# Low parts of weights split half a tile later, two products that start without new weights, and a table pass moved behind a convolution's first step, in a hybrid decoder layer on one core

## The chip, the cores and the metric

The kernel runs on one core of a Trainium2 chip. The metric is the device time of one execution in microseconds (us). Engines are named as in the profile: PE multiplies matrices, DVE and ACT work element by element, POOL does side work, SP issues transfers (DMA). Each engine takes its instructions strictly in the order of its own queue, and waits on semaphores for what other engines and transfers deliver.

## The reference

One layer of a decoder trunk on 512 tokens of width 1024, in float32:

```python
h = rms_norm(x, norm_g[0]); proj = h @ w_in          # one projection, split into all branches
y_a = rglru_mixer(lru_x, lru_g, conv_w, conv_b, ...)  # width-4 depthwise conv, gates, linear recurrence, gelu
y_b = nsa_mixer(...)                                  # sparse attention
y_c = gla_mixer(...)                                  # log_alpha = log_sigmoid(lr @ wa2 + ba) / 16, then chunks
merged = gates[0] * (y_a @ w_branch[0]) + gates[1] * (y_b @ w_branch[1]) + gates[2] * (y_c @ w_branch[2])
x = x + rms_norm(merged @ w_out, norm_g[1])
h = rms_norm(x, norm_g[2])
gt, up = jnp.split(h @ w_ffn_in, 2, axis=-1)          # D_FF = 2816
x = x + rms_norm((jax.nn.silu(gt) * up) @ w_ffn_out, norm_g[3])
```

## The kernel before

**Products in split precision.** Every operand of a product is split into a high part in a reduced format (fp32r) and a low part, the rest. A weight tile of 128x1024 comes from DRAM into a buffer `wraw`. ACT copies it into `whi` (the high part, a CAST of about 1.05 us), DVE subtracts that from `wraw` into `wlo` (the low part, about 1.2 us). Then `mm3` (lines 121 to 124) makes three products per pair: high with high (L122), high with low weights (L123), low with high (L124). The pool `wpool` holds three buffers each of `wraw`, `whi` and `wlo`. A `wraw` buffer can be loaded again once DVE has made its low part; a `whi` or `wlo` buffer once PE has used it.

**The recurrent branch.** A loop over `cp` = 0 to 3 handles two of eight channel groups at a time: a projection `px` (`stream_t`), `conv(cp, px)`, a second projection `pgl`, `gate_products(cp)` and a third stream `pm`. `conv` (L988 to L1005) begins on ACT with two scaled copies of `px` into `xc`, goes on with three DVE steps per half (L1000), casts the result to `xh` on ACT (L1002), and subtracts on DVE into `xl` (L1004). The products `rips` of `gate_products` need `xh` and `xl`. Into this loop the logarithms of the GLA decays are woven: `z_products`, `z_exp` and `z_log` run in the `pm` stream of `cp` = 2, and `z_log` (L1072) is four activations that need another activation table. `z_scan` reads their result in the `pgl` stream of `cp` = 3.

**The FFN, first product.** `w_ffn_in` is applied by a seven-product (Strassen-Winograd) scheme, P1 to P7, on quarters. The list `seq` names the products in order, `winograd(s)` does one of them, twelve matmuls into the PSUM bank A, B or C, and `after(op, q)` evacuates it: `keep` is a copy by ACT, `y_half` (L1719) an addition by DVE, `act(q)` (L1751) the product with the silu. `winograd` also prepares weights two tiles ahead: `f_cast(i)` at even s, `f_lo(i)` at odd s. The last two products, P7 and P4 of q = 21, go into the same bank A, so P4 may start only when DVE has read P7 out.

**The FFN, second product.** `w_ffn_out` is applied with another seven-product scheme. The list `stream` orders the weight tiles: a0, b0, a1, b1, ... a10, b10 (`tile_a`, `tile_b`), then pairs of rows and columns. `tile_a(k)` loads two quarters of `w_ffn_out`; `tile_b(k)` loads one block of row sums from `rows_d` and computes the other block on DVE from the raw a tile (L1806). `split_u` casts on ACT and makes the low part on DVE (L1779, L1782). `weights()` hands out the next tile and, by `ahead(i + 3)`, sets up the tile two places later. `use(bank, ...)` does six matmuls of 512 columns with half a tile; every tile serves two such uses. At k = 0, tile a0 is used once between P6 and P7 and once between P7 and P4; from then on step k of the loop (L1933) does two uses of a(k) and two of b(k).

**The order of the work.** PE, DVE, ACT and POOL run in the order in which the program is written (`manual_schedule`); the transfers on SP are put in order by the scheduler. `late` is a list of low parts put off; before the change it is used only near the end (L1996 and L2005). `fetch2(k)` loads a block `r2` for `second(k - 2)` from a pool of three buffers, `gb3` is a vector of gains, and `xr` are the eight loads of the residual (L1970).

```python
    def f_lo(i):
        if i < len(floads):
            raw, hi = fq[i]
            lo = wpool.tile([128, 1024], F32R, name="wlo")
            v_.tensor_tensor(lo, raw, f(hi), op=OP.subtract)
            fq[i] = hi, lo
```

Of the kernel before, what the change touches and what calls it, by code (L numbers as in the profile page):

```python
# [10 lines left out]
F32 = mybir.dt.float32  # L11
# [51 lines left out]
def hybrid_block_kernel(ctx, tc, x, rel_table, norm_g, w_in, conv_w, conv_b, lru_w_gates, lru_b_gates,  # L63
# [924 lines left out]
    def conv(cp, pss):  # L988

        xh = lp.tile([128, 2, S], F32R, name="xh")  # L990
        xl = lp.tile([128, 2, S], F32R, name="xl")
        xc = lp.tile([128, 2, S], F32, name="xc")
        for j, ps in enumerate(pss):
            ct = 2 * cp + j
            a_.activation(xc[:, j], ps, AF.Identity, scale=par[:, 24 + ct:25 + ct], bias=par[:, 32 + ct:33 + ct])
        for j, ps in enumerate(pss):
            ct = 2 * cp + j
            for jj in (2, 1, 0):
                d = 3 - jj
                v_.scalar_tensor_tensor(xc[:, j, d:], ps[:, :S - d], par[:, jj * 8 + ct:jj * 8 + ct + 1],  # L1000
                                        xc[:, j, d:], op0=OP.mult, op1=OP.add)
            a_.copy(xh[:, j], xc[:, j])  # L1002
        for j in range(2):
            v_.tensor_tensor(xl[:, j], xc[:, j], f(xh[:, j]), op=OP.subtract)  # L1004
        L.update(xc=xc, xh=xh, xl=xl)  # L1005
# [76 lines left out]
    for cp in range(4):  # L1082
# [4 lines left out]
        conv(cp, px)  # L1087
# [8 lines left out]
        if cp == 0:  # L1096
            lru_params()
        pm = stream_t(Y[:2], chain(lambda: lru_tanh(cp), *([z_products] if cp == 2 else [])),
                      chain(lambda: lru_exp(cp), *([z_exp, z_log] if cp == 2 else [])))
# [510 lines left out]
    fq = []  # L1610

    def f_cast(i):
        if i < len(floads):
            raw = floads[i]()
            hi = wpool.tile([128, 1024], F32R, name="whi")
            a_.copy(hi, raw)  # L1616
            fq.append([raw, hi])
        else:
            ahead(i - len(floads) + 1)

    def f_lo(i):
        if i < len(floads):
            raw, hi = fq[i]
            lo = wpool.tile([128, 1024], F32R, name="wlo")
            v_.tensor_tensor(lo, raw, f(hi), op=OP.subtract)  # L1625
            fq[i] = hi, lo
# [140 lines left out]
    late = []  # L1767

# [7 lines left out]
    def split_u(raw, n=1024):  # L1776
        hi = wpool.tile([128, 1024], F32R, name="whi")
        lw = wpool.tile([128, 1024], F32R, name="wlo")
        a_.copy(hi[:, :n], raw[:, :n])  # L1779

        def low():
            v_.tensor_tensor(lw[:, :n], raw[:, :n], f(hi[:, :n]), op=OP.subtract)  # L1782

        if late:
            late.append(low)
        else:
            low()
        return hi, lw

# [5 lines left out]
    def tile_a(k):  # L1795

        t = last["a"] = raw_tile()
        sy.dma_start(t[:, 0:512], wsrc(k, 0))
        sy.dma_start(t[:, 512:1024], wsrc(NK + k, 1))
        return split_u(t)  # L1800

    def tile_b(k):

        t, ab = raw_tile(), last["a"]
        sy.dma_start(t[:, 0:512], rows_d[k * 128:k * 128 + 128, 512:1024])
        v_.tensor_tensor(t[:, 512:1024], ab[:, 0:512], ab[:, 512:1024], op=OP.subtract)  # L1806
        return split_u(t)
# [30 lines left out]
    def use(bk, ls, sl, w, hf, k, tts=(0, 1)):  # L1838
        wh, wl = [t[:, hf * 512:hf * 512 + 512] for t in w]
        for tt in tts:  # L1840
            c = slice(tt * 128, tt * 128 + 128)
            mm3(bk[tt], ls[:, 0, sl, c], ls[:, 1, sl, c], wh, wl, k == 0, k == NK - 1)

# [14 lines left out]
    w = weights()  # L1858
    use(p5, LS1[0], 2, w, 1, 0)
# [3 lines left out]
    use(p2, LS1[0], 1, w, 0, 0)  # L1863
    winograd(len(seq) - 1)
    after(*seq[-1])
    a_.activation(cst[:, 2:3], cst[:, 0:1], AF.Sqrt)
# [8 lines left out]
    def fetch2(k):  # L1875
        if k < NK - 1:
            raw2[k] = fr.tile([128, 3, 256], F32, name="r2", bufs=3)
# [42 lines left out]
    def store(tb, hf):  # L1920
# [3 lines left out]
        (sy if hf else a_).dma_start(out[0, tb * 128:(tb + 1) * 128, c], o)  # L1924
# [6 lines left out]
    fetch2(0)  # L1931
    fetch2(1)
    for k in range(NK):  # L1933
# [20 lines left out]
        fetch2(k + 2)  # L1954
# [35 lines left out]
    for p in range(NP - 3):  # L1990
# [3 lines left out]
        if p == 1:  # L1994

            late.append(None)  # L1996
# [7 lines left out]
        if p == 2:  # L2004
            for low in late[1:]:  # L2005
                low()
# [51 lines left out]
```

## Time and profile before

| what | value |
|---|---|
| median of 3 runs | 1201.88 us (1201.55 to 1203.12) |
| the profiled execution, its own time | 1202.26 us |
| its span in the trace | 1200.6 us |
| mean granted PE clock | 0.996 |
| PE busy | 1180.5 us, 98% |
| DVE, ACT, POOL busy | 726.3, 607.0, 256.6 us |

The span runs from the first to the last instruction that the profiler saw; the time also holds what lies around it, 1.7 us here. In the timeline each row gives the start, the duration, the engine, the line of the kernel, the operation, and in brackets how long the engine idled before it and what ended that. In the rows of stretches the columns are: the stretch, its length, the busy time of PE, of PE's weight loads, of DVE, ACT and POOL with their instruction counts, the granted clock of PE (1.00 is full), the DMA share and GB/s.

### The profile page before, as it was taken

The page shows a single profiled execution, that of the slowest core. Times are in us where ns is not written, and L with a number is a line of the kernel's source. Part 1 is how long each engine was busy: PE and PEld are TensorE (multiplying, and loading weights), DVE is VectorE, ACT ScalarE, POOL GpSimd, SP SyncE. Part 2 cuts the span into 40 slices and gives each one's busy share as a digit, 9 for nine tenths or more (in the row PEclk, how much of TensorE's full clock was granted, in tenths as well). Part 3 has the DMA queues.
Part 4 walks back from the last instruction along what each step waited for, and adds up shares of the span by engine and source line. Part 5 has one row for each costly group of instructions (what it writes and reads, how often), then busy time and mean ns, then how long its engine had stood idle before and what let it go on. Part 6 is the DMA issues. An engine that isn't in the chain of part 4 may idle for free. (4 is left out here: it accounts for less than half of the span.)

```text
span 1200.6 us, 19226 instructions
## 1 busy us (share of the span) xinstructions
PE 1180.5 (98%) x7114; PEld 1009.9 (84%) x7114; DVE 726.3 (60%) x1417; ACT 607.0 (51%) x1165; POOL 256.6 (21%) x327
## 2 busy tenths in 40 slices
PE   9999999999999999999999999999999999989996
PEld 7898888888888878888888888887989999987785
DVE  6615556555467769465544353446786777765777
ACT  5326656565387677453434233234455565644553
POOL 1224555566213213222122222200000000000000
PEclk9999999999999999999999999999999999999999
DMA  8872765551469947885487989944246667667753
GB/s 259 236 217 83 195 222 196 179 163 40 115 153 228 246 151 215 202 201 150 132 203 179 212 196 236 214 149 134 85 123 189 207 202 212 197 193 239 244 184 123
DMA packets 203743, 219.30 MB, mean 183 GB/s; under 512 B 29170, under 2 KB 169694, under 8 KB 201424
## 3 DMA queue, kind: packets, MB, share of 16 engines
q1 hardware_dynamic: 189120, 170.87, 46.7%
q0 software_dynamic: 13936, 46.14, 18.3%
q8 instruction: 56, 0.92, 0.3%
q10 hardware_dynamic: 592, 1.05, 0.2%
q14 instruction: 39, 0.32, 0.1%
HBM read 209.83 MB, written 77.41 MB: 239 GB/s over the span
## 5 line engine op out<-in xcount | busy, mean ns | idle before, releaser
L92 DVE TENSOR_TENSOR wlo<-wraw,whi 128x1024 fp32r<-128x1024 f32 x91 | 111.8, 1233 | 113.6 <-ACT whi L91 86.9
L91 ACT CAST whi<-wraw 128x1024 fp32r<-128x1024 f32 x113 | 117.9, 1048 | 118.7 <-PE gps L897 29.6
L870 POOL COPY tick<-whi 128x1 f32<-128x1 f32 x76 | 53.8, 708 | 340.4 <-ACT whi L91 340.4
L894 PE MATMUL gps<-hh,whi 128*128 128x512 f32 x320 | 126.0, 394 | 0.0
L897 PE MATMUL gps<-hl,whi 128*128 128x512 f32 x320 | 124.5, 389 | 0.0
L1625 DVE TENSOR_TENSOR wlo<-wraw,whi 128x1024 fp32r<-128x1024 f32 x67 | 81.9, 1222 | 14.5 <-ACT whi L1616 14.0
L676 DVE COPY psb<-ptp 128x512 f32<-128x512 f32 (+2 forms) x72 | 45.4, 631 | 64.2 <-PE ptp L672 60.5
L637 ACT ACTIVATE p<-p,mx 128x384 f32<-128x384 f32 (+3 forms) x128 | 68.7, 539 | 26.7 <-DVE mx L635 26.5
L894 PE MATMUL gps<-hh,wlo 128*128 128x512 f32 x320 | 79.1, 389 | 0.0
L1616 ACT CAST whi<-wraw 128x1024 fp32r<-128x1024 f32 x67 | 70.3, 1049 | 13.4 <-DMA wraw<-t_d 12.0
L651 POOL TENSOR_TENSOR p<-p,sc 128x256 f32<-128x256 f32 (+3 forms) x64 | 76.5, 1217 | 1.9
L894 PE MATMUL gps<-yh,whi 128*128 128x512 f32 x192 | 74.9, 390 | 0.0
L897 PE MATMUL gps<-yl,whi 128*128 128x512 f32 x192 | 74.7, 389 | 0.0
L122 PE MATMUL gps<-hh,whi 128*128 128x512 f32 (+1 forms) x176 | 73.4, 418 | 0.8 <-DVE hl L316 0.8
L894 PEld LDWEIGHTS gps<-hh,wlo 128*128 128x128 f32 x320 | 60.1, 188 | 12.5
L894 PEld LDWEIGHTS gps<-hh,whi 128*128 128x128 f32 x320 | 60.1, 188 | 12.4
L897 PEld LDWEIGHTS gps<-hl,whi 128*128 128x128 f32 x320 | 60.1, 188 | 12.3
L122 PE MATMUL gps<-whi,hh 128*128 128x512 f32 (+1 forms) x192 | 69.9, 364 | 0.0
L124 PE MATMUL gps<-whi,hl 128*128 128x512 f32 (+1 forms) x192 | 68.1, 354 | 0.0
L123 PE MATMUL gps<-wlo,hh 128*128 128x512 f32 (+1 forms) x192 | 68.0, 354 | 0.0
L124 PE MATMUL gps<-hh,wlo 128*128 128x512 f32 (+1 forms) x176 | 65.7, 374 | 0.0
L123 PE MATMUL gps<-hl,whi 128*128 128x512 f32 (+1 forms) x176 | 65.5, 372 | 0.0
(442 smaller groups left out, 3061.8 us busy)
## 6 DMA issues: line engine op xcount, KB each, us to landing
wraw<-in_w_in_dram SPq DMA_DIRECT2D x44, 512.0 KB, 6.4
t_d<-in_w_ffn_in_dram SPq DMA_DIRECT2D x32, 704.0 KB, 8.0
wraw<-t_d SPq DMA_DIRECT2D x72, 256.0 KB, 3.2
wraw<-in_w_ffn_in_dram SPq DMA_DIRECT2D x70, 256.0 KB, 3.8
wraw<-in_w_in_dram SPq DMA_DIRECT2D x64, 256.0 KB, 4.5
t_d<-in_w_ffn_in_dram POOLq DMA_DIRECT2D x16, 704.0 KB, 9.2
rows_d<-in_w_ffn_out_dram POOLq DMA_DIRECT2D x22, 512.0 KB, 5.2
t_d<-t_d POOLq DMA_DIRECT2D x16, 704.0 KB, 8.2
```

Source lines behind the costliest of these rows:

```text
L91: a_.copy(hi, raw)
L92: lo_eng.tensor_tensor(lo, raw, f(hi), op=OP.subtract)
L122: pe.matmul(ps, lh, rh, start=first, stop=False)
L123: pe.matmul(ps, lh, rl, start=False, stop=False)
L124: pe.matmul(ps, ll, rh, start=False, stop=last)
L637: a_.activation(o, o, AF.Exp, scale=-1.0, bias=mx[:, br, gi:gi + 1], accum_out=sm[:, br, gi:gi + 1])
L651: g_.tensor_tensor(o, o, sc[:, br][:, :, None].to_broadcast([128, 2, n]), op=OP.mult)
L870: g_.tensor_copy(tick, f(hi[:, 0, 0:1]))
L894: pe.matmul(ps[n], part_[:, k, c], ah[:, kk], start=kk == 0 and part_ is h, stop=kk == 7 and part_ is l)
L897: pe.matmul(ps[n], h[:, k, c], al[:, kk], start=False, stop=False)
L1616: a_.copy(hi, raw)
L1625: v_.tensor_tensor(lo, raw, f(hi), op=OP.subtract)
```

## The change

- **z_log.** The four logarithms of the decays and their table load leave the `pm` stream of `cp` = 2. `conv` takes a new argument `then`, called behind its first step (the two scaled copies on ACT), and for `cp` = 3 that is `z_log`.
- **Low parts half a tile later.** `split_u` no longer emits the low part; it appends it to `late`. `lows()` empties `late`. It is called at the start of `f_lo`, at the end of each `use` (after its matmuls), and once ahead of the first `use`.
- **tile_a and tile_b.** `tile_a(k)` now allocates both raw tiles, issues the load for b as well, and subtracts the computed half of b (L1806 before) ahead of the low part of a. `tile_b(k)` only casts.
- **The change of products.** The first two uses take tile a0 as `done[0]`, and `weights()` is no longer called ahead of them. The setting up of b0 moves to the call of `winograd` for P7, that of a1 behind P4.
- **Smaller moves.** The table load for Sqrt with its dummy activation moves from behind P4 to the end of the a/b loop. `fetch2` runs one step later from a pool of four buffers, and the two fetches ahead of the loop go. All stores but the last go out by SP, the last by ACT.

```diff
@@ -985,7 +985,7 @@
         v_.tensor_tensor(gwl, raw, f(gwh), op=OP.subtract)
         L["gw"] = gwh, gwl
 
-    def conv(cp, pss):
+    def conv(cp, pss, then=None):
 
         xh = lp.tile([128, 2, S], F32R, name="xh")
         xl = lp.tile([128, 2, S], F32R, name="xl")
@@ -993,6 +993,8 @@
         for j, ps in enumerate(pss):
             ct = 2 * cp + j
             a_.activation(xc[:, j], ps, AF.Identity, scale=par[:, 24 + ct:25 + ct], bias=par[:, 32 + ct:33 + ct])
+        if then:
+            then()
         for j, ps in enumerate(pss):
             ct = 2 * cp + j
             for jj in (2, 1, 0):
@@ -1084,7 +1086,7 @@
             px = stream_t(hT, lambda: y_split(0), lambda: gate_weights(0))
         else:
             px = stream_t(hT, lru_root, chain(lambda: lru_scan(cp - 1), lambda: gate_weights(cp)))
-        conv(cp, px)
+        conv(cp, px, z_log if cp == 3 else None)
         if cp == 0:
             pgl = stream_t(hT, lambda: y_split(1), chain(lambda: y_split(2), lambda: y_split(3)))
         elif cp == 3:
@@ -1096,7 +1098,7 @@
         if cp == 0:
             lru_params()
         pm = stream_t(Y[:2], chain(lambda: lru_tanh(cp), *([z_products] if cp == 2 else [])),
-                      chain(lambda: lru_exp(cp), *([z_exp, z_log] if cp == 2 else [])))
+                      chain(lambda: lru_exp(cp), *([z_exp] if cp == 2 else [])))
         for j in range(2):
             merge_mul(cp, j, pm[j])
     pq = stream_t(hT, chain(lru_root, lambda: lru_scan(3)))
@@ -1608,8 +1610,15 @@
 
     floads += [lambda s=s: quarters(seq[s:s + 2]) for s in range(0, len(seq), 2)]
     fq = []
+    late = []
+
+    def lows():
+        while late:
+            late.pop(0)()
 
     def f_cast(i):
+        if i >= len(floads) + 2:
+            return
         if i < len(floads):
             raw = floads[i]()
             hi = wpool.tile([128, 1024], F32R, name="whi")
@@ -1619,6 +1628,7 @@
             ahead(i - len(floads) + 1)
 
     def f_lo(i):
+        lows()
         if i < len(floads):
             raw, hi = fq[i]
             lo = wpool.tile([128, 1024], F32R, name="wlo")
@@ -1764,8 +1774,6 @@
 
     HP = []
     raws = [0]
-    late = []
-
     def raw_tile():
         i = raws[0]
         raws[0] += 1
@@ -1781,11 +1789,9 @@
         def low():
             v_.tensor_tensor(lw[:, :n], raw[:, :n], f(hi[:, :n]), op=OP.subtract)
 
-        if late:
-            late.append(low)
-        else:
-            low()
+        late.append(low)
         return hi, lw
+
 
     def wsrc(r, c):
         return dap(w_ffn_out, r * 128 * D + c * 512, [[D, 128], [1, 512]])
@@ -1794,17 +1800,17 @@
 
     def tile_a(k):
 
-        t = last["a"] = raw_tile()
+        t, tb_ = raw_tile(), raw_tile()
         sy.dma_start(t[:, 0:512], wsrc(k, 0))
         sy.dma_start(t[:, 512:1024], wsrc(NK + k, 1))
+        sy.dma_start(tb_[:, 0:512], rows_d[k * 128:k * 128 + 128, 512:1024])
+        v_.tensor_tensor(tb_[:, 512:1024], t[:, 0:512], t[:, 512:1024], op=OP.subtract)
+        last["b"] = tb_
         return split_u(t)
 
     def tile_b(k):
 
-        t, ab = raw_tile(), last["a"]
-        sy.dma_start(t[:, 0:512], rows_d[k * 128:k * 128 + 128, 512:1024])
-        v_.tensor_tensor(t[:, 512:1024], ab[:, 0:512], ab[:, 512:1024], op=OP.subtract)
-        return split_u(t)
+        return split_u(last["b"])
 
     def pair(src):
         def load(p):
@@ -1840,6 +1846,7 @@
         for tt in tts:
             c = slice(tt * 128, tt * 128 + 128)
             mm3(bk[tt], ls[:, 0, sl, c], ls[:, 1, sl, c], wh, wl, k == 0, k == NK - 1)
+        lows()
 
     for s in range(len(seq) - 2):
         winograd(s)
@@ -1855,15 +1862,15 @@
         after(*seq[s])
 
     p2, p5 = [[p.tile([128, 512], F32, name="acc", tag=n) for _ in range(2)] for p, n in ((pa, "a"), (pt, "pt"))]
-    w = weights()
-    use(p5, LS1[0], 2, w, 1, 0)
+    lows()
+    use(p5, LS1[0], 2, done[0], 1, 0)
     y_half(2 * NK - 1, 0, "C", "u2")
     winograd(len(seq) - 2)
     after(*seq[-2])
-    use(p2, LS1[0], 1, w, 0, 0)
+    use(p2, LS1[0], 1, done[0], 0, 0)
     winograd(len(seq) - 1)
     after(*seq[-1])
-    a_.activation(cst[:, 2:3], cst[:, 0:1], AF.Sqrt)
+    weights()
     fictx.close()
     fctx = ExitStack()
     fr = fctx.enter_context(tc.tile_pool(name="ffr", bufs=1, side="right"))
@@ -1874,7 +1881,7 @@
 
     def fetch2(k):
         if k < NK - 1:
-            raw2[k] = fr.tile([128, 3, 256], F32, name="r2", bufs=3)
+            raw2[k] = fr.tile([128, 3, 256], F32, name="r2", bufs=4)
             sy.dma_start(raw2[k], raw2_d[:, k])
 
     def second(k):
@@ -1921,15 +1928,13 @@
         c = slice(hf * 512, hf * 512 + 512)
         o = C[tb][:, c]
         v_.scalar_tensor_tensor(o, gained[tb, hf], rss[tb][1][:, 0:1], xres[tb, hf], op0=OP.mult, op1=OP.add)
-        (sy if hf else a_).dma_start(out[0, tb * 128:(tb + 1) * 128, c], o)
+        (a_ if (tb, hf) == (1, 1) else sy).dma_start(out[0, tb * 128:(tb + 1) * 128, c], o)
 
     def add(o, x_, y, op=OP.add):
         v_.tensor_tensor(o, x_, y, op=op)
 
     p3, p1 = [[pg.tile([128, 512], F32, name="acc", tag="g") for _ in range(2)] for _ in range(2)]
     p4, p6, p7 = p2, p5, p3
-    fetch2(0)
-    fetch2(1)
     for k in range(NK):
         if k:
             w = weights()
@@ -1951,7 +1956,11 @@
             second(k - 2)
         if k == 4:
             second(NK - 1)
-        fetch2(k + 2)
+        if k == 0:
+            fetch2(0)
+        fetch2(k + 1)
+        if k == NK - 1:
+            a_.activation(cst[:, 2:3], cst[:, 0:1], AF.Sqrt)
     for p in range(NP):
         w = weights()
         for k in range(2 * p, min(2 * p + 2, NK)):
@@ -1993,7 +2002,6 @@
             use(p7, LS2[k], 1, w, k % 2, k)
         if p == 1:
 
-            late.append(None)
             ahead(turns[0] + 3)
         if p in (0, 1):
             add(C[2 + p][:, c1], p6[p], C[2 + p][:, c1])
@@ -2002,8 +2010,6 @@
             gain(2 + p, 1)
             mean(2 + p)
         if p == 2:
-            for low in late[1:]:
-                low()
             store(2, 0)
             store(2, 1)
             root(3)
```

ACT around the logarithms, in the recurrent branch at the end of `cp` = 2 and the start of `cp` = 3 (`yf` holds the decays, `a` is the recurrence's root, `gwh` the gate weights, `xc` and `xh` are the convolution's). Before:

```order
L1072 ACT_TABLE_LOAD
L1072 ACTIVATE yf<-yf,cst 128x512 x4
L91 CAST whi<-wraw 128x1024
L1047 ACT_TABLE_LOAD
L1047 ACTIVATE a_4787<-a_4787 128x1024
L91 CAST whi<-wraw 128x1024
L984 CAST gwh<-gwr 128x512
L995 ACTIVATE xc<-gps,par 128x512 x2
L1002 CAST xh<-xc 128x512 x2
```

Of the change:

```order
L91 CAST whi<-wraw 128x1024
L1049 ACT_TABLE_LOAD
L1049 ACTIVATE a_4787<-a_4787 128x1024
L91 CAST whi<-wraw 128x1024
L984 CAST gwh<-gwr 128x512
L995 ACTIVATE xc<-gps,par 128x512 x2
L1074 ACT_TABLE_LOAD
L1074 ACTIVATE yf<-yf,cst 128x512 x4
L1004 CAST xh<-xc 128x512 x2
```

The load of the table and the four logarithms now stand behind `xc` and ahead of `xh`; the two casts of weights, the root and `xc` stand ahead of them.

DVE at the FFN's change of products (`am<-fy,fsg` is `act`, the two `fy` are `y_half` for q = 21, the 512-wide `wraw` row is the computed half of a b tile, L1782 and L1790 are low parts of tiles a and b). Before:

```order
L1782 TENSOR_TENSOR wlo<-wraw,whi 128x1024
L1751 SCALAR_TENSOR_TENSOR am<-fy,fsg 128x512
L1806 TENSOR_TENSOR wraw<-wraw 128x512
L1782 TENSOR_TENSOR wlo<-wraw,whi 128x1024 x2
L1719 TENSOR_TENSOR fy<-wc,u_10699 128x256
L1719 TENSOR_TENSOR fy<-wa,p_10586 128x256
L1806 TENSOR_TENSOR wraw<-wraw 128x512
L1782 TENSOR_TENSOR wlo<-wraw,whi 128x1024
L1751 SCALAR_TENSOR_TENSOR am<-fy,fsg 128x512
```

Of the change:

```order
L1807 TENSOR_TENSOR wraw<-wraw 128x512
L1790 TENSOR_TENSOR wlo<-wraw,whi 128x1024
L1761 SCALAR_TENSOR_TENSOR am<-fy,fsg 128x512
L1729 TENSOR_TENSOR fy<-wc,u_10702 128x256
L1729 TENSOR_TENSOR fy<-wa,p_10586 128x256
L1790 TENSOR_TENSOR wlo<-wraw,whi 128x1024
L1807 TENSOR_TENSOR wraw<-wraw 128x512
L1790 TENSOR_TENSOR wlo<-wraw,whi 128x1024 x2
L1761 SCALAR_TENSOR_TENSOR am<-fy,fsg 128x512
```

The two low parts (b0 and a1) that stood ahead of the additions `fy` stand behind them; ahead of a0's low part there is now b0's subtraction.

SP where the loads of tile a3 stand (`gb` is the vector of gains, `r` the blocks of `fetch2`, `xr` the residual). Before:

```order
L1798 DMA wraw<-in_w_ffn_out_dram 128x512
L1871 DMA gb_10766<-in_norm_g_dram 128x1024
L1878 DMA r_10775<-raw_d 128x768
L1878 DMA r_10777<-raw_d 128x768
L1878 DMA r_10801<-raw_d 128x768
L1799 DMA wraw<-in_w_ffn_out_dram 128x512
L1805 DMA wraw<-rows_d 128x512
L1798 DMA wraw<-in_w_ffn_out_dram 128x512
L1799 DMA wraw<-in_w_ffn_out_dram 128x512
L1970 DMA xr_11337<-x_d 128x512
L1970 DMA xr_11339<-x_d 128x512
L1970 DMA xr_11341<-x_d 128x512
```

Of the change:

```order
L1804 DMA wraw<-in_w_ffn_out_dram 128x512
L1878 DMA gb_10767<-in_norm_g_dram 128x1024
L1885 DMA r_10796<-raw_d 128x768
L1885 DMA r_10798<-raw_d 128x768
L1885 DMA r_10839<-raw_d 128x768
L1805 DMA wraw<-in_w_ffn_out_dram 128x512
L1806 DMA wraw<-rows_d 128x512
L1885 DMA r_10883<-raw_d 128x768
L1804 DMA wraw<-in_w_ffn_out_dram 128x512
L1805 DMA wraw<-in_w_ffn_out_dram 128x512
L1979 DMA xr_11337<-x_d 128x512
L1804 DMA wraw<-in_w_ffn_out_dram 128x512
```

The two halves of a3 still have the gains and three `r` blocks between them; of the eight `xr` loads one, where there were three, is left ahead of a5.

## Rows read from the trace of the kernel before

**Rows 1.** The page's first lines: span, and busy time per engine.

```profile
span 1200.6 us, 19226 instructions
...
PE 1180.5 (98%) x7114; PEld 1009.9 (84%) x7114; DVE 726.3 (60%) x1417; ACT 607.0 (51%) x1165; POOL 256.6 (21%) x327
```

**Rows 2.** Waits of PE: who waited, for whom, total, times, longest.

```profile
PE wa L1707 <- DVE fy L1719: 3.1, 1, 3.1
PE acc L123 <- DVE wlo L1782: 1.3, 3, 0.8
PE rips L123 <- DVE xl L1004: 1.3, 1, 1.3
```

**Rows 3.** Timeline of ACT around the logarithms.

```profile
430.50 1.28 ACT L1072 ACT_TABLE_LOAD   x1
431.79 2.56 ACT L1072 ACTIVATE yf<-yf,cst 128x512 f32<-128x512 f32 x4
434.26 1.03 ACT L91 CAST whi<-wraw 128x1024 fp32r<-128x1024 f32 x1
```

**Rows 4.** Timeline of DVE in the same place.

```profile
435.33 1.23 DVE L92 TENSOR_TENSOR wlo<-wraw,whi 128x1024 fp32r<-128x1024 f32 x1 [4.48 <-ACT whi L91]
...
444.09 4.53 DVE L1000 SCALAR_TENSOR_TENSOR xc<-gps,par,xc 128x511 f32<-128x511 f32 x6
448.54 1.51 DVE L1004 TENSOR_TENSOR xl<-xc,xh 128x512 fp32r<-128x512 f32 x2
```

**Rows 5.** Timeline of PE in the same place.

```profile
436.70 0.39 PE L894 MATMUL gps<-hh,whi 128*128 128x512 f32 x1
...
447.58 0.39 PE L122 MATMUL rips<-xh,gwh 128*128 128x512 f32 x1
449.27 0.50 PE L123 MATMUL rips<-xl,gwh 128*128 128x512 f32 x1 [1.30 <-DVE xl L1004]
...
449.84 0.39 PE L122 MATMUL rips<-xh,gwh 128*128 128x512 f32 x1
```

**Rows 6.** Stretches: all engines, granted clock, DMA share.

```profile
1071.51:1083.68 12.17, 8.97 (x44) 7.53 (x43) 5.34 (x8) 3.84 (x5) 0.00 (x0) 0.86 0.56 181
1079.33:1082.05 2.72, 2.72 (x12) 2.72 (x13) 0.54 (x1) 0.00 (x0) 0.00 (x0) 0.50 0.27 96
1090.51:1128.01 37.50, 35.58 (x145) 26.32 (x144) 24.91 (x26) 17.30 (x20) 0.00 (x0) 1.00 0.81 274
1139.21:1172.14 32.93, 32.93 (x146) 27.02 (x144) 26.44 (x32) 19.34 (x30) 0.00 (x0) 1.00 0.61 197
447.60:452.00 4.40, 3.10 (x14) 2.26 (x13) 3.96 (x6) 3.29 (x5) 1.59 (x2) 1.00 0.00 0
```

**Rows 7.** Timeline of DVE at the FFN's change of products.

```profile
1070.72 1.22 DVE L1782 TENSOR_TENSOR wlo<-wraw,whi 128x1024 fp32r<-128x1024 f32 x1
...
1077.38 1.23 DVE L1782 TENSOR_TENSOR wlo<-wraw,whi 128x1024 fp32r<-128x1024 f32 x1 [1.90 <-ACT whi L1779]
...
1079.19 0.68 DVE L1806 TENSOR_TENSOR wraw<-wraw 128x512 f32<-128x512 f32 x1
...
1086.31 0.69 DVE L1751 SCALAR_TENSOR_TENSOR am<-fy,fsg 128x512 f32<-128x512 f32 x1
```

**Rows 8.** Timeline of ACT in the same place and at tile a3.

```profile
1082.29 0.38 ACT L1742 ACTIVATE fsg<-wa 128x256 f32<-128x256 f32 x1 [4.94 <-PE wa L1707]
1082.69 1.28 ACT L1866 ACT_TABLE_LOAD   x1
...
1095.56 1.05 ACT L1779 CAST whi<-wraw 128x1024 fp32r<-128x1024 f32 x1 [3.60 <-DMA wraw<-in_w_ffn_out_dram]
```

**Rows 9.** Timeline of SP: the second half of tile a3.

```profile
1088.86 0.54 SPq L1799 DMA_DIRECT2D wraw<-in_w_ffn_out_dram  x1
```

**Rows 10.** Timeline of PE: the second product of tiles a0 and a3.

```profile
1071.99 0.50 PE L123 MATMUL acc<-wlo,ls 128*128 128x512 f32 x1
...
1097.92 0.51 PE L123 MATMUL acc<-wlo,ls 128*128 128x512 f32 x1 [0.76 <-DVE wlo L1782]
```

## The prediction, made before the changed kernel had run

> **What bounds the kernel.** The first lines of the page come first [rows 1]: PE is busy 1180.5 of 1200.6 us, so only what PE waits for can be won, and little of it. The list of PE's waits then says for whom [rows 2]. Three entries touch the change: one wait of 3.1 us for `fy`, the additions that free bank A between P7 and P4; three waits, 1.3 us together, for low parts of `w_ffn_out`; one of 1.3 us for `xl` of the convolution. This list keeps only clear gaps. What a place really costs is read from stretches [rows 6]: a quiet one, 1139.21 to 1172.14, has 24 uses (144 products of 512 columns) in 32.93 us, 1.372 us per use. Everything below is measured against that pace.
>
> **Part A, the logarithms.** Behind the third `pgl` stream PE starts `rips` at 447.58; the fourth product starts at 449.84 [rows 5]. Three products should take 3 x 0.229 = 0.69 us and take 2.26, so this place loses 1.58 us. The reason lies well before it: ACT loads a table at 430.50 and does the four logarithms until 434.26, and only then casts a weight tile [rows 3]; DVE idles 4.48 us for that cast [rows 4], and its whole queue (a low part, the root's product, the scans, six convolution steps from 444.09, `xl` at 448.54) comes late.
>
> With the logarithms gone from there, the cast starts at 430.50 and DVE's queue moves 3.76 us forward, unless something else holds it. The candidate is `xc`, which needs the whole of `px`; PE begins the next stream at 436.70 [rows 5], so `xc` runs from about 436.9 to 438.3, while the convolution's steps would start at 444.09 - 3.76 = 440.33: no hold. The moved block, 1.28 + 2.48 = 3.76 us, now occupies ACT from 438.3 to 442.1. Behind it waits `xh`, whose first half needs three steps of DVE, done at 440.33 + 4.53/2 = 442.6. So the block just fits, and the first half of `xl` ends near 448.54 - 3.76 + 0.75 = 445.5; PE wants it at 447.8. Spare 2.3 us. The readers of the logarithms, the scans, come in the `pgl` stream behind `xl` in DVE's queue, later still. **Gain 1.58 us.**
>
> **Part B, the change of products.** From the first use of a0 (1071.51) to the end of the first use of b0 (1083.68) there are three uses and two Winograd products. A Winograd product is 12 matmuls; P4 took 2.72 us at a granted clock of 0.50 [rows 6], so 1.36 at full clock. Undisturbed the stretch takes 3 x 1.372 + 2 x 1.36 = 6.84 us; it took 12.17, at a mean clock of 0.86: 5.3 lost. Bank A is read late because DVE's queue holds b0's and a1's low parts ahead of `fy`, and a1's cast comes so late that its low part runs from 1077.38 on [rows 7].
>
> In the changed order the additions stand ahead of both. P7 then ends about 1075.2, `fy` needs 0.42 and is done near 1075.9, and PE meanwhile has 1.37 us of a0's second use. P4 starts without a wait. What is late next is a0's own low part: b0's subtraction now stands ahead of it and takes 0.61 at the queue's pace (0.68 as a row [rows 7]). Before, that low part ran from 1070.72 and PE's product started right behind it at 1071.99 [rows 7, 10], so this product slips 0.6 us. It already was 0.4 late. So 1.0 of the 5.3 stays. b0's low part, now behind `fy`, is done near 1077.1, and PE wants it at 1078.1. a1 is tighter: its cast stands behind the silu of P4, which ends near 1078.6; cast 1.05 and low part 1.23 make 1080.9, and PE wants it at 1081.0. In its favour the Sqrt table load, 1.28 us behind that silu [rows 8], is gone. **Gain 4.2 us**, bounds 3.4 (0.8 lost at a1) and 5.3.
>
> **Part C, tiles a2 to b7.** From 1090.51 to 1128.01 there are again 24 uses, and they took 37.50 us: 4.57 lost [rows 6]. The start of it is a3: its second half is issued at 1088.86 [rows 9], its cast starts at 1095.56 when it has landed [rows 8], PE's low product follows at 1097.92 [rows 10] where 1090.51 + 4 x 1.372 + 0.23 = 1096.2 was due. With the 0.11 that the two products behind a wait take longer (0.57 for 0.46, [rows 5]), a3 costs 1.85; the other 2.7 is spread over the tiles after it, each late because each buffer is released late.
>
> a3 stays late, I think. Its second half still goes out behind the gains and three `r` blocks, and these go out behind DVE's `act`, which was at 1086.31 [rows 7]. In the new order `act` follows the low parts of a1 and b1, casts ending near 1079.6 and 1080.6, low parts near 1080.9 and 1082.0: it moves 4.4 us forward, and PE's place moves 4.2 forward. With the same 6.7 us from issue to cast, the wait stays at 1.7. Bounds: 0, if the transfers ahead are thinner, and 2.5, if b2's rows, which now go out just ahead, cost one more 256 KB block.
>
> The spread part should go. Before, b's subtraction, cast and low part came one behind the other after a's low part (0.6 + 1.05 + 1.15); now the subtraction lies beside a's cast, and b's cast needs nothing of DVE: b is ready 1.7 us earlier. Ahead of a5 one `xr` load stands instead of three, at a DMA share of 0.81 [rows 6]. **Gain 4.57 - 1.7 = 2.9 us**, bounds 0 and 4.6.
>
> **What costs nothing.** The Sqrt load (1.28 and a dummy of 0.2) now lies at the end of the a/b loop, where ACT's casts wait for PE to free a `whi`; with that cover gone it costs 1.5. The last store goes out by ACT instead of SP: an issue is under 0.6 us on either [rows 9], so +-0.3. `fetch2` one step later still leaves three steps of the loop, 16 us, between fetch and use.
>
> **Sum.** 1.58 + 4.2 + 2.9 = 8.7. The profiled execution took 1202.26, so 1193.6; the median of the runs lies 0.38 lower, and I take 1193.3.
>
> **A rule weighed.** Before, a wait of 3.1 us was followed by half clock, 0.50 of full, which is 1.2 instead of 2.4 GHz, through all of P4 [rows 2, 6]; a wait of 1.30 was not, the stretch behind it is at 1.00 [rows 5, 6]. The sum counts the lost clock as won back and nothing for the new waits. The Trainium skill (TensorE: Matmul & The Clock Gate, Part 1) says that the throttled state is the default and that activity releases it. By that rule the wait that stays at a3 could bring half clock again; by the rows alone it brings nothing.
>
> **Rivals.**
> 1. *a3 comes in time.* The loads ahead of it could drain faster, since fewer `xr` run. For it: the whole stretch is then as quiet as the later one. Against: the gains and `r` blocks alone are 1.6 MB. Time 1193.3 - 1.7 = 1191.6; the 0.6 at a0 may vanish too, 1191.0.
> 2. *Part C gains nothing*: raw buffers, released half a tile later in DVE's queue, keep every tile late. Time 1193.3 + 2.9 = 1196.2.
> 3. *Half clock behind a3's wait.* One Winograd product at half clock lost 1.36, so 1194.7. The rule is the one above; the row of 1.30 speaks against.
> 4. *Slower.* One mechanism: the ring of three raw buffers in the a/b loop. A tile's load waits for the low part three tiles back. If that low part comes a whole use later (1.37 us) and the load takes longer than the lead left, every tile is late. It decides once the release comes less than about 6.7 us (issue to cast, [rows 8, 9]) before PE's need. The 18 tiles a2 to b10 at 0.8 each, the size of the wait at a3's low part [rows 10], make 14.4 instead of the 4.57: 1202.26 - 1.58 - 4.2 + 9.8 = 1206.3. Against it: DVE does not wait for PE between low parts, it idles much, so half a tile later in the program is seldom later in time.
> 5. *Nothing happens.* A, B or C merely shift waits to the next place, as a1 (0.1 us of spare) would: 1200 to 1204. The order of DVE's queue says that the low parts do move, so little weight.
>
> **Chances.** Forecast 0.53, rival 1 0.15, rival 2 0.16, rival 3 0.07, rival 4 0.04, rival 5 0.05. From this kernel a measurement can tell about 0.2%, 2.4 us, from no change. Faster by more: 0.53 + 0.15 + 0.16 + 0.07 = 0.91, less 0.01 for mixtures, 0.90; same 0.06; slower 0.04. The range takes in rivals 1 to 3 with their bounds: from 1190.3 (the high bounds of B and C, and 0.2 for the spread of runs) to 1197.2 (rival 2, the low bound of B, and 0.2).
>
> **What would show it.** Right: no gap of PE at `xl`, and `xh` cast right behind the logarithms; no gap at P4 and full clock through it; a slip of about 0.6 at a0's low part; one wait of 1 to 2 us at a3; 24 uses from k = 2 in 34 to 35 us. Wrong: waits for low parts through k = 4 to 7 (rival 2), a clock under 1.00 behind a3 (rival 3), waits that go on to b10 (rival 4).

## The result, and the profile after

The changed kernel took 1194.52 us (median of 6 runs, 1193.05 to 1197.26), the kernel before on the same chip 1202.02 (6 runs). The ratio is 0.9941, with a 95% interval of 0.9927 to 0.9955: faster by 0.6%. The forecast was 1193.3, its range 1190.3 to 1197.2. The profiled execution of after is one of these runs:

| what | before | after |
|---|---|---|
| the profiled execution, its own time | 1202.26 us | 1194.62 us |
| its span | 1200.6 us | 1192.9 us |
| mean granted PE clock | 0.996 | 0.998 |

The page's first lines, answering to [rows 1]:

```profile
span 1192.9 us, 19219 instructions
...
PE 1176.3 (99%) x7114; PEld 1009.0 (85%) x7114; DVE 727.1 (61%) x1417; ACT 607.5 (51%) x1165; POOL 257.0 (22%) x327
```

The waits of PE (who, for whom, total, times, longest), answering to [rows 2]. The entries for `fy` and `xl` are gone. The one for a `whi` of `w_ffn_out`, which [rows 2] leaves out, has grown from 0.5 to 1.5 us. Of before, and the two of after:

```profile
PE acc L122 <- ACT whi L1779: 0.5, 1, 0.5
```

```profile
PE acc L123 <- DVE wlo L1790: 1.7, 3, 0.8
PE acc L122 <- ACT whi L1787: 1.5, 1, 1.5
```

The stretches, with the columns of [rows 6]: from the first use of a0 to the end of the first use of b0, and the 24 uses from k = 2, with a3's wait in them and a clock of 1.00:

```profile
1069.98:1077.96 7.98, 7.28 (x44) 6.24 (x43) 4.13 (x6) 2.50 (x4) 0.00 (x0) 1.00 0.71 221
1084.78:1120.59 35.81, 33.53 (x145) 26.94 (x144) 25.79 (x28) 18.02 (x21) 0.00 (x0) 1.00 0.86 294
```

With these rows the 7.7 us of the span fall into four pieces. The first use of a0 comes at 1069.98 instead of 1071.51: 1.53 (the same code reaches it at 1069.36 and 1069.18 in c1 and c2 below, so this one reading has a spread of some 0.8). The change of products takes 7.98 instead of 12.17: 4.19. The 24 uses take 35.81 instead of 37.50: 1.69. The 0.3 that is left lies at other places, mostly behind these.

**The logarithms.** ACT, answering to [rows 3], and PE, answering to [rows 5]:

```profile
430.70 1.03 ACT L91 CAST whi<-wraw 128x1024 fp32r<-128x1024 f32 x1
...
439.06 2.56 ACT L1074 ACTIVATE yf<-yf,cst 128x512 f32<-128x512 f32 x4
442.93 0.62 ACT L1004 CAST xh<-xc 128x512 fp32r<-128x512 f32 x1 [1.30 <-DVE xc L1002]
```

```profile
447.66 0.39 PE L122 MATMUL rips<-xh,gwh 128*128 128x512 f32 x1
...
448.34 0.39 PE L122 MATMUL rips<-xh,gwh 128*128 128x512 f32 x1
```

The cast starts at 430.70 instead of 434.26. The moved block (its table load, 1.28 us, and these four) sits between `xc` and `xh`, and behind it ACT even waits 1.30 for DVE, so it holds nothing up. PE does three products in 448.34 - 447.66 = 0.68, where before it took 2.26 [rows 5]: 1.58 less at this spot.

**The change of products.** DVE, answering to [rows 7], and then PE:

```profile
1069.19 0.68 DVE L1807 TENSOR_TENSOR wraw<-wraw 128x512 f32<-128x512 f32 x1
1069.80 1.22 DVE L1790 TENSOR_TENSOR wlo<-wraw,whi 128x1024 fp32r<-128x1024 f32 x1
...
1073.96 0.42 DVE L1729 TENSOR_TENSOR fy<-wa,p 128x256 f32<-128x256 f32 x1 [2.01 <-PE wa L1717]
...
1080.41 0.69 DVE L1761 SCALAR_TENSOR_TENSOR am<-fy,fsg 128x512 f32<-128x512 f32 x1
```

```profile
1071.07 0.50 PE L123 MATMUL acc<-wlo,ls 128*128 128x512 f32 x1 [0.70 <-DVE wlo L1790]
...
1075.14 0.28 PE L1717 MATMUL wa<-hh,whi 128*128 128x256 f32 x1
...
1091.90 0.51 PE L122 MATMUL acc<-whi,ls 128*128 128x512 f32 x1 [1.52 <-ACT whi L1787]
1093.16 0.50 PE L123 MATMUL acc<-wlo,ls 128*128 128x512 f32 x1 [0.75 <-DVE wlo L1790]
```

DVE is now idle when P7 ends and reads it out at once (1073.96). P4 starts at 1075.14 with no gap in front. The price is at 1071.07: a0's low part, behind b0's subtraction, is 0.70 late. The two lowest rows are a3, the only tile from k = 2 on that PE waits for, apart from 0.2 us at the very end. SP and the chain of waits say why a3 is late:

```profile
1079.39 0.33 SPq L1806 DMA_DIRECT2D wraw<-rows_d  x1
...
1081.55 1.79 SPq L1885 DMA_DIRECT2D r<-raw_d  x3
1083.38 0.65 SPq L1805 DMA_DIRECT2D wraw<-in_w_ffn_out_dram  x1
```

```profile
1083.38 7.32 DMA wraw<-in_w_ffn_out_dram
...
1090.80 1.05 ACT whi L1787
```

The second half of a3 goes out at 1083.38 behind b2's rows, its own first half, the gains and three `r` blocks, and takes 7.32 us to land.

### The profile page after: what moved, and what is told of

Its sections match the earlier page's. It is cut to its first block, busy times and chain, and to the rows that moved or that the text cites. A ratio compares the mean times of both kernels' runs of the same rounds, so it can differ in the third digit from the quotient of the medians.

```text
span 1192.9 us, 19219 instructions
## 1 busy us (share of the span) xinstructions
PE 1176.3 (99%) x7114; PEld 1009.0 (85%) x7114; DVE 727.1 (61%) x1417; ACT 607.5 (51%) x1165; POOL 257.0 (22%) x327
## 4 chain that ended last, share of the span: by engine, by line
PE 93%; DVE 3%; DMA 1%; ACT 1%; issue 1%; SPq 0%; DVEq 0%; ACTq 0%
PE gps L894 19%; PE gps L897 10%; PE gps L122 8%; PE gps L123 7%; PE gps L124 7%; PE wa L1717 6%; PE ops L694 4%; PE s L626 3%; PE wa L1720 3%; PE ptp L672 3%; PE wc L1717 3%; PE acc L123 2%; PE acc L124 2%; PE acc L122 2%; PE gps L164 2%; PE wb L1717 1%
```

## The experiments

In all of them "the 24 uses" is the stretch from the first use of a2, and what it loses is counted against 32.96 us, its length in the two runs (e6 and e7, below) in which it has no wait. After loses 35.81 - 32.96 = 2.85 there.

**e1: the logarithms alone**, in the kernel before.

```diff
-    def conv(cp, pss):
+    def conv(cp, pss, then=None):
...
+        if then:
+            then()
...
-        conv(cp, px)
+        conv(cp, px, z_log if cp == 3 else None)
...
-chain(lambda: lru_exp(cp), *([z_exp, z_log] if cp == 2 else []))
+chain(lambda: lru_exp(cp), *([z_exp] if cp == 2 else []))
```

> The kernel before, with the logarithms of the decays moved behind the convolution's first step and nothing else. Theory (ACT's queue held one cast, and so DVE's whole queue, 3.76 us back): the 1.30 us wait of PE for xl is gone, the first four products of rips follow each other at 0.23 us, and the span is 1.5 to 1.6 us shorter than before's 1200.6, the FFN's waits unchanged (3.1 at P4, 4.6 lost over the 24 uses from k = 2). Rival (xc or the moved block holds xh, so that xl is late again): the wait stays at 0.5 us or more.

It took 1200.74, with a span of 1199.0 instead of 1200.6: 1.6 less. `rips` runs without a gap, as in after: its first product starts at 447.55, the fourth at 448.24, 0.69 later and not 2.26. What stays is the wait at P4, in the list of waits:

```profile
PE wa L1709 <- DVE fy L1721: 3.1, 1, 3.1
```

and the stretch behind P4, at a clock of 0.62:

```profile
1080.36:1084.65 4.29, 4.29 (x14) 3.40 (x14) 1.19 (x2) 2.80 (x4) 0.00 (x0) 0.62 0.02 5
```

The first use of a0 comes at 1069.79, 1.72 earlier than before, 1.57 of it at `rips`: that is Part A's gain on its own. That the span fits so well is partly luck, for the FFN was expected to stay as it was and did not. Its two stretches:

```profile
1069.79:1082.92 13.13, 9.93 (x45) 8.20 (x43) 5.35 (x8) 4.76 (x7) 0.00 (x0) 0.77 0.52 169
1090.08:1126.48 36.40, 35.42 (x145) 26.32 (x144) 24.17 (x26) 16.04 (x19) 0.00 (x0) 1.00 0.81 278
```

The first is 0.96 longer than before's 12.17, the second 1.10 shorter than before's 37.50. The first is longer for the clock: half clock goes on for seven products behind P4 here, and for one behind P4 before, so the same wait of 3.1 us costs a different length of half clock from run to run. The kernel before, run once beside it, took 1201.26, only 0.52 more: it is the place that shows Part A, not the total.

**e2: the later `weights()` alone**, in the kernel before: the two uses of a0 take it as it is, and a1 is set up behind P4.

```diff
-    w = weights()
-    use(p5, LS1[0], 2, w, 1, 0)
+    use(p5, LS1[0], 2, done[0], 1, 0)
...
-    use(p2, LS1[0], 1, w, 0, 0)
+    use(p2, LS1[0], 1, done[0], 0, 0)
...
+    weights()
     a_.activation(cst[:, 2:3], cst[:, 0:1], AF.Sqrt)
```

> The kernel before, with weights() moved from ahead of the first use of a0 to behind P4, low parts still made at once. Theory (what matters is that a1's low part no longer stands ahead of the additions fy in DVE's queue): the wait of 3.1 us at P4 and the half clock go, the stretch from the first use of a0 to the end of the first use of b0 falls from 12.2 to about 7.5 us; the 24 uses from k = 2 stay slow, 36.5 to 37.5. Rival (the low parts put off by half a tile do it): the stretch stays near 12.

It took 1202.12, span 1200.4: no gain, and for the 24 uses the expectation missed. Its two stretches, and two rows of DVE's timeline:

```profile
1074.16:1081.78 7.62, 7.53 (x44) 6.16 (x43) 3.53 (x6) 2.60 (x4) 0.00 (x0) 1.00 0.77 244
1088.80:1128.16 39.36, 35.98 (x146) 26.17 (x144) 25.62 (x28) 17.86 (x20) 0.00 (x0) 1.00 0.79 268
```

```profile
1077.24 1.23 DVE L1782 TENSOR_TENSOR wlo<-wraw,whi 128x1024 fp32r<-128x1024 f32 x1 [1.11 <-ACT whi L1779]
...
1086.04 0.69 DVE L1751 SCALAR_TENSOR_TENSOR am<-fy,fsg 128x512 f32<-128x512 f32 x1
```

The wait at P4 is gone, and the first stretch is 4.55 shorter than before's 12.17. Of the two low parts it was a1's that held `fy`: b0's, the first of the two rows, still runs ahead of it here, and P4 does not wait. But the 24 uses take 1.86 longer than before's 37.50. The second row says why: `act` still stands behind b1's low part, for whose cast DVE idles 1.11 us just before, and `act` releases the transfers in front of a3. It runs 1088.80 - 1086.04 = 2.76 ahead of the 24 uses, where before had 1090.51 - 1086.31 = 4.20 and after has 1084.78 - 1080.41 = 4.37. So PE came earlier to a3 and the load did not.

The first stretch starts 2.65 later than before, at a place that the edit does not touch. At `rips` PE waits 0.34 and 1.62 us, where before it waited 1.30 [rows 5], and this time half clock follows:

```profile
451.00:454.40 3.40, 3.40 (x10) 2.63 (x9) 3.11 (x4) 3.38 (x7) 2.20 (x4) 0.51 0.18 10
```

So "no gain" in the total says little; the two stretches are the result.

**e3: the reverse**, in after: `weights()` ahead of the first use again, all else as changed.

```diff
     lows()
+    weights()
     use(p5, LS1[0], 2, done[0], 1, 0)
...
-    weights()
     fictx.close()
```

> The changed kernel, with weights() back ahead of the first use, low parts still half a tile late. Theory (order of DVE's queue): b0's and a1's low parts stand ahead of fy again, P4 waits 3 to 4 us with half clock behind it, the stretch is 12 to 13 us. Rival (the late low parts suffice): P4 doesn't wait and the stretch stays at 8.0.

It took 1197.21, span 1195.5, 2.6 more than after's (a single run, within the spread of after's own; the places decide). Its wait at P4, and the two stretches:

```profile
PE wa L1717 <- DVE fy L1729: 3.2, 1, 3.2
```

```profile
1069.36:1082.17 12.81, 8.88 (x45) 7.49 (x43) 5.27 (x7) 3.63 (x5) 0.00 (x0) 0.87 0.51 172
1088.97:1123.20 34.23, 33.48 (x145) 26.94 (x144) 25.35 (x27) 17.88 (x20) 0.00 (x0) 1.00 0.92 315
```

With a1 ahead of `fy` in DVE's queue the wait of P4 is back in full, with its half clock (0.87), late low parts or not. The first stretch is 4.83 longer. But a3 now loses 34.23 - 32.96 = 1.27 instead of 2.85, since PE comes to it later: a third of what P4's wait had cost was waited out again at a3 once it was gone.

**e4: b's subtraction back in `tile_b`**, in after.

```diff
-        v_.tensor_tensor(tb_[:, 512:1024], t[:, 0:512], t[:, 512:1024], op=OP.subtract)
-        last["b"] = tb_
+        last["a"], last["b"] = t, tb_
         return split_u(t)
...
-        return split_u(last["b"])
+        t, tb_ = last["a"], last["b"]
+        v_.tensor_tensor(tb_[:, 512:1024], t[:, 0:512], t[:, 512:1024], op=OP.subtract)
+        return split_u(tb_)
```

> The changed kernel, with the computed half of a b tile subtracted when the b tile is set up, as before, instead of with the a tile. Theory: the slip of 0.7 us at a0's low part goes (stretch 8.0 to 7.3), and behind a3's wait the b tiles are late again, since subtraction, cast and low part follow one another: waits of 0.1 to 0.5 us at b3 to b7 and 36.3 to 37 us for the 24 uses from k = 2 instead of 35.8. Rival (fewer transfers of xr ahead of a5 are what cured the tiles behind a3): the 24 uses stay at 35.8 with one wait, at a3.

It took 1199.54, span 1197.8, 4.9 more than after. The two stretches and the one behind a7's wait, then a7 itself on PE:

```profile
1069.24:1076.63 7.39, 7.30 (x44) 6.25 (x43) 4.12 (x7) 2.60 (x4) 0.00 (x0) 1.00 0.76 242
1083.45:1125.07 41.62, 37.11 (x145) 27.57 (x144) 25.05 (x27) 18.35 (x22) 0.00 (x0) 0.96 0.80 273
1118.00:1121.50 3.50, 3.45 (x9) 2.75 (x10) 2.26 (x3) 2.73 (x3) 0.00 (x0) 0.55 0.23 75
```

```profile
1116.79 0.50 PE L122 MATMUL acc<-whi,lsf 128*128 128x512 f32 x1 [1.42 <-ACT whi L1787]
```

The slip at a0 is gone, the first stretch 0.59 shorter: that is its price. The 24 uses come out at 41.62 and not at 36 to 37: losses of 0.1 to 0.4 at each tile from b3 to b6 but a5, as in before, then a wait of 1.42 and 0.76 at a7, with half clock behind it (0.55). ACT's row for b3's cast names what it waits for, the subtraction:

```profile
1092.34 1.05 ACT L1787 CAST whi<-wraw 128x1024 fp32r<-128x1024 f32 x1 [2.02 <-DVE wraw L1813]
```

So the place of b's subtraction is what cured the tiles right behind a3. a7 is another case: the second half of its load goes out at 1108.69, behind such a sequence on DVE, and takes 6.85 to land. The rival isn't wholly excluded there, since the scheduler put two `xr` ahead of a5 in this kernel, where after has one and before three.

**e5: the gains and the `r` blocks on POOL's queue**, in after.

```diff
-    sy.dma_start(gb3, dap(norm_g, 3 * D, [[0, 128], [1, D]]))
+    g_.dma_start(gb3, dap(norm_g, 3 * D, [[0, 128], [1, D]]))
...
-            sy.dma_start(raw2[k], raw2_d[:, k])
+            g_.dma_start(raw2[k], raw2_d[:, k])
```

> The changed kernel, with the gains and the r blocks issued from POOL's queue instead of SP's; bytes and due times unchanged. Theory (a3's second half stands behind 1.6 MB in SP's queue): it is issued right behind the first half, and PE's waits at a3 (1.52 and 0.75, 2.8 us lost) go, 24 uses from k = 2 in about 33 us. Rival (the 16 transfer engines are full in that stretch, whichever queue the bytes come from): a3 still lands 6 us or more after its issue and 1 us or more of the wait stays.

It took 1199.61, span 1197.7, 4.8 more than after's. PE at a3 and b3, the stretch behind b3's wait, and the transfers issued from 1079 to 1100 (count, size, median us from issue to landing):

```profile
1090.85 0.50 PE L123 MATMUL acc<-wlo,ls 128*128 128x512 f32 x1 [0.36 <-DVE wlo L1790]
1097.04 0.79 PE L122 MATMUL acc<-whi,ls 128*128 128x512 f32 x1 [3.41 <-ACT whi L1787]
```

```profile
1098.30:1103.00 4.70, 4.70 (x11) 3.73 (x12) 4.59 (x5) 2.35 (x4) 0.54 (x1) 0.50 0.79 260
```

```profile
wraw<-in_w_ffn_out_dram SPq DMA_DIRECT2D x6, 256.0 KB, 7.6
r<-raw_d POOLq DMA_DIRECT2D x4, 384.0 KB, 10.3
```

a3's second half goes out right behind its first and is almost in time (0.36). But the loads of `w_ffn_out` still take 7.6 us, the `r` blocks 10.3, and now b3 is 3.41 late, with half clock behind it. SP, freed of the `r` blocks, sent three `xr` ahead of b3's rows. So the theory holds for a3 alone, and the 24 uses take 40.80 instead of its 33; of the rival the slow landing came true and the wait at a3 did not. The DMA share is 0.92 from 1081 to 1096, and 0.92 from 1081 to 1091 in after. An emptier queue does not help where the DMA engines are that full; fewer bytes in front should.

**e8: only the gains out of the way**, in after: 512 KB less in front of a3.

```diff
-    sy.dma_start(gb3, dap(norm_g, 3 * D, [[0, 128], [1, D]]))
...
         if k == NK - 1:
+            sy.dma_start(gb3, dap(norm_g, 3 * D, [[0, 128], [1, D]]))
             a_.activation(cst[:, 2:3], cst[:, 0:1], AF.Sqrt)
```

> The changed kernel, with the load of the gains (512 KB) moved behind the a/b loop. Theory (bytes ahead of a3's second half): at the 0.37 MB per us at which the r blocks landed before, 512 KB are 1.4 us, so the 2.8 us lost at a3 become 1.4, and the 24 uses from k = 2 take 34.4 instead of 35.8. Rival (a3 is late because its raw buffer is released half a tile later): the wait stays at 2.5 us or more.

**e6: the `r` blocks two steps later as well**: e8, and

```diff
-        if k == 0:
-            fetch2(0)
-        fetch2(k + 1)
+        if k:
+            fetch2(k - 1)
+        if k == NK - 2:
+            fetch2(k)
```

> The changed kernel, with the gains behind the a/b loop and the r blocks fetched two steps later than in it. Theory (bytes ahead): only one r block is left between the halves of a3, 0.4 MB or 1.1 us instead of 4.5, so the wait at a3 goes wholly, and the 24 uses from k = 2 take 33.0 to 33.3; span near 1190.1. Rival (late release): the wait stays. A second one: the r blocks now come too late for second(k), and low parts behind it in DVE's queue wait: new waits of PE at k = 3 to 6.

e8 took 1192.50 (span 1190.8), e6 1192.13 (span 1190.4). The 24 uses of e8, a3 on PE in e8, and the 24 uses of e6:

```profile
1084.57:1118.48 33.91, 33.26 (x145) 26.94 (x144) 25.79 (x28) 18.00 (x21) 0.00 (x0) 1.00 0.89 305
```

```profile
1091.04 0.50 PE L123 MATMUL acc<-wlo,ls 128*128 128x512 f32 x1 [0.65 <-DVE wlo L1790]
```

```profile
1084.66:1117.62 32.96, 32.96 (x145) 27.02 (x144) 25.88 (x28) 18.22 (x21) 0.00 (x0) 1.00 0.94 321
```

Without the gains a3's second half is issued at 1082.91 and lands at 1088.58, 5.67 us later instead of 7.32, and a3 loses 0.95: the 24 uses take 33.91, where 34.4 was expected. With one `r` block in front of it instead of three it loses nothing, and no new wait comes at k = 3 to 6: the transfers in front of a3 are its wait, by their bytes and by the time that SP takes to issue them.

**e7: e6, and b0's subtraction behind a0's low part**, for the slip that e4 had priced.

```diff
-        v_.tensor_tensor(tb_[:, 512:1024], t[:, 0:512], t[:, 512:1024], op=OP.subtract)
         last["b"] = tb_
-        return split_u(t)
+        def rest():
+            v_.tensor_tensor(tb_[:, 512:1024], t[:, 0:512], t[:, 512:1024], op=OP.subtract)
+        if k:
+            rest()
+        out_ = split_u(t)
+        if not k:
+            late.append(rest)
+        return out_
```

> As the one before, and the computed half of b0 alone is subtracted behind a0's low part. Theory: the wait at a3 (2.8 us) and the slip at a0 (0.7 us, less the 0.1 that was there before) both go: 1194.5 - 2.8 - 0.6 = 1191.1 us. Rival: what is won at a3 comes back as waits at later tiles, 1193 to 1195.

It took 1191.09 (median of 4 runs, 1190.66 to 1191.40) against 1202.20 before (7 runs): 0.9902, interval 0.9886 to 0.9919. It beats both kernels. Its two stretches:

```profile
1069.57:1076.95 7.38, 7.29 (x45) 6.24 (x43) 4.12 (x7) 2.61 (x4) 0.00 (x0) 1.00 0.72 235
1083.78:1116.74 32.96, 32.96 (x145) 27.02 (x144) 26.63 (x28) 19.24 (x22) 0.00 (x0) 1.00 0.95 322
```

The first stretch is 0.60 shorter than after's, the second 2.85. (Two other differences cancel: the first stretch starts 0.41 earlier, and 0.5 more passes behind the last product. To that extent the exact hit of the expectation is luck.) Of waits of this product of the FFN the list has only 0.2 us, at its end. Its runs also lie within 0.7 us of each other, where those of after spread over 4.2.

**c1 and c2: after once more**, unchanged, for that spread.

> The changed kernel once more, unchanged. Its six runs spread from 1193.05 to 1197.26, twice as far as those of before. Theory (PE's wait at a3, some 2.3 us in two parts, is at times followed by half clock, as at a7 in the kernel with the subtraction in tile_b): the runs fall into a group near 1193 to 1194.6 and some 1.4 to 3 us above it, with a lower mean clock in the upper ones; where the profile has half clock it stands behind a3. Rival (spread elsewhere): upper runs without a lower clock, or half clock in another place.

> The same, a second profile: what the wait at a3 costs in another execution (2.84 us by the first), and whether half clock follows it.

c1: 1195.53 (median of 6 runs, 1194.82 to 1197.16), ratio 0.9943, interval 0.9929 to 0.9957. The times do not fall into two groups. Of c1, a3 on PE and the 24 uses:

```profile
1092.12 0.50 PE L122 MATMUL acc<-whi,ls 128*128 128x512 f32 x1 [2.37 <-ACT whi L1787]
```

```profile
1084.15:1120.82 36.67, 33.55 (x146) 26.94 (x145) 26.57 (x28) 18.98 (x22) 0.00 (x0) 1.00 0.86 295
```

Of c2 (1194.91, one run) the same, and the stretch behind a3's wait:

```profile
1090.61 0.49 PE L122 MATMUL acc<-whi,ls 128*128 128x512 f32 x1 [1.02 <-ACT whi L1787]
1091.87 0.50 PE L123 MATMUL acc<-wlo,ls 128*128 128x512 f32 x1 [0.77 <-DVE wlo L1790]
```

```profile
1092.00:1096.00 4.00, 4.00 (x11) 3.13 (x12) 4.00 (x5) 1.28 (x2) 0.00 (x0) 0.57 0.69 220
1083.99:1120.89 36.90, 35.11 (x145) 28.07 (x144) 26.56 (x28) 19.26 (x22) 0.00 (x0) 0.95 0.86 299
```

In c1 a3's wait is longer than in after's first profile and the clock stays at 1.00; in c2 it is shorter, and half clock follows (0.57). The 24 uses lose 3.71 and 3.94: a3 has two prices, a wait that varies and a clock that sometimes falls.

Why the wait varies can be read from the load of a3's second half. The chain of waits has its issue and the time to its landing, in c1 and then in c2:

```profile
1083.35 7.58 DMA wraw<-in_w_ffn_out_dram
```

```profile
1082.91 6.50 DMA wraw<-in_w_ffn_out_dram
```

| run | issued ahead of a2's first product | issue to landing | lost by the waits at a3 |
|---|---|---|---|
| before | 1.65 | 6.60 | 1.85 |
| after | 1.40 | 7.32 | 2.82 |
| c1 | 0.80 | 7.58 | 3.67 |
| c2 | 1.08 | 6.50 | 2.32, and 1.6 by the clock |
| e8 | 1.66 | 5.67 | 0.91 |

The loss is what the products of a3 take beyond 0.229 us each, the pace of [rows 6]. In each row it is the landing time less the lead less 3.1, within 0.02; e1, e3, e4 and e5 fit as closely, and e2, where PE has already waited 0.3 at b2, loses 0.4 less. So two things set the wait: the time to landing, and how early SP issues the load. To issue the gains and the three `r` blocks in front of it SP took 1.75 us before, 2.17 in after, 2.76 in c1 and 2.50 in c2, so it too differs between executions of one kernel.

## Why the prediction was right, and where its sum was off

- **Part A, 1.58: 1.58 at `rips` in after, 1.57 alone (e1).** The step as it was put, ACT's cast 3.76 forward and DVE's queue with it, held: the cast moved 3.56, the convolution's steps came at 440.53 where 440.33 was forecast.
- **Part B, 4.2: 4.19.** The additions ahead of the low parts end the wait at P4 and its half clock; e2 and e3 show from both sides that it is this place in DVE's queue, and e2 that a1's low part was the one that mattered. That it hit to 0.01 is luck: the prediction's own 5.3 less 1.0 is 4.3, and a Winograd product at full clock takes 1.44 (P4 of after runs from 1075.14 to 1076.58), not 1.36. The slip of 0.6 at a0's low part came, and e4 and e7 price it at 0.59 and 0.60. a1, forecast with 0.1 us to spare, came without a wait.
- **Part C, 2.9: 1.69. This term was mis-sized.** Its spread part held: no tile behind a3 waits, which is worth 2.66 for the 2.7 that the prediction had counted, and e4 brings the waits of b3 to b6 back when the subtraction goes back. What failed is "the wait stays at 1.7", which rested on "the same 6.7 us from issue to cast": one profile's time, taken as fixed. (By the prediction's own count a3 cost 1.85, not 1.7.) `act` did move ahead with PE, 5.90 against 5.73. But the second half of a3 went out only 5.48 earlier than before (1083.38 for 1088.86), 0.25 less than PE's 5.73, and from issue to cast passed 7.42 for 6.70, 0.72 more. 1.85 + 0.25 + 0.72 = 2.82, of the 2.85 that was lost. The upper bound of 2.5 named a cause, b2's rows ahead of a3, and was too low. That the transfers in front set this wait is shown by e8 and e6; that the rows have a part in it is argued, and was not run alone. The landing time of one profile can't show it: it was 6.60, 7.29 and 7.35 us where the rows had gone out over 6 us ahead of a3's first half (before, e1, e3), and 7.32, 7.58, 6.50 and 6.38 where they went out 1.1 us ahead (after, c1, c2, e4). With SP's issues counted in, from the issue of the gains to the landing, it was 8.4 to 9.1 and 9.0 to 10.4, on average 0.7 more: the rows fit as a cause, but the spread is as large as their effect.
- **What costs nothing, and the sum.** Nothing is left over at the Sqrt load, the last store or `fetch2`: the 0.3 us outside the three parts are a gain. 8.7 was forecast for the span, 7.7 came; the miss is Part C's 1.2, less that.
- **Rivals.** 1 (a3 in time) did not come by itself; e6 made it, and with the slip gone (e7) it gave 1191.1, where the rival had said 1191.0, close in part by luck, as said there. 2 and 4 fall with the tiles from k = 4 on, which don't wait. 5 is half true for one part alone: e2 moved a wait from P4 to a3. **3 (half clock behind a3's wait) was given 0.07 and does occur:** not in the profiles of after and c1, but in that of c2. "The row of 1.30 speaks against" was one row taken for a rule: in e2 half clock followed at that very place, `rips`, behind 0.34 and 1.62. The Trainium skill's sentence in TensorE: Matmul & The Clock Gate, Part 1, that the default state is throttled and activity releases it, leaves room for it: c2 agrees (clock 0.57 behind waits of 1.02 and 0.77), the profiles of after and c1 show no half clock there.

Open is what decides whether half clock follows a3's wait, and why SP's issues and the landing vary, by which the first gap at a3 varies between 1.0 and 2.4 us in the same kernel. That these two make the spread of after's runs is in part argued, from e7's small spread. Run by run there is only the mean clock: 0.995 and 0.996 in after's two slowest runs (1197.26 and 1196.88), 0.997 and 0.998 in the other four. So lost clock has its part in the spread; at which place it was lost is not shown.

## What to carry to other kernels

In an engine's queue, put the step that frees a bank (or releases a transfer) ahead of preparations that are needed later; it costs the preparation its slack, which the trace can price beforehand. When a wait is removed, everything after it is wanted earlier, and the next load that was just late becomes the new wait: follow its issue, and the bytes in front of it, before counting the gain as kept. Where the DMA engines are full, another queue does not help; a later start for what is not yet needed does.

## What the runs showed of the hardware

- Half clock (1.2 of 2.4 GHz) can follow short waits, and not always: behind 1.02 and 0.77 (c2, a3), 1.42 and 0.76 (e4, a7) and 0.34 and 1.62 (e2, `rips`) it came, behind 1.52 and 0.75 (after), 2.37 and 0.76 (c1), 0.65 (e8) and 1.30 (before, `rips`) it did not. Behind P4's wait of 3.1 to 3.2 it came in all three runs that have it (before, e1, e3); it went on for one product behind P4 in before and e3, for seven in e1.
- A wait costs more than its gap. In after, a3's two waits are 2.27 us together and cost 2.85; the product right behind each takes 0.51 and 0.50 where a product without a wait takes 0.39 and starts 0.23 after the last, so that a wait also ends this overlap.
- The time from issue to landing of the same 256 KB load went with what was in front of it: 5.67 us in e8 without the gains, 6.38 to 7.58 in the four profiles with them (after, c1, c2, e4), and 7.62 in e5, where the blocks went through another engine's queue.
